# Layer 1 grouped-query attention: the two context query tiles of a head pair as one step

## The chip, the cores and the metric

The kernel runs on one core of one Trainium2 chip. The metric is the device time of one execution in microseconds (us); the median of three runs is quoted. Beside the timed runs there is one profiled execution, from which all traces here come. Engines are named as in the profile: PE (TensorE), DVE (VectorE), ACT (ScalarE), POOL (GpSimd), SP (the queue that issues most DMAs).

## The reference

A two-layer trunk of 512 latent tokens and 256 context tokens, 1024 channels wide. Each layer holds a mixer with four parallel branches (Fourier, convolution, grouped-query attention, differential attention) that are gated, summed and projected, and a SwiGLU sub-layer. What matters here:

```python
# grouped-query attention: 8 query heads of 64, 2 key/value heads
def gqa_attend(q, k, v):
    s = jnp.einsum("bhgqd,bhkd->bhgqk", q, k) * (HEAD_DIM ** -0.5)
    p = jax.nn.softmax(s, axis=-1)
    return jnp.einsum("bhgqk,bhkd->bhgqd", p, v)
# context stream (layer 1 only): reads only itself        -> 256 keys
# latent stream: reads all latent and all context tokens  -> 768 keys

def conformer_conv(z, w, bias, ln_g, ln_b):
    a, g = jnp.split(z, 2, axis=-1)
    u = a * jax.nn.sigmoid(g)
    y = depthwise_conv(u, w, 31 taps) + bias
    return jax.nn.silu(layer_norm(y, ln_g, ln_b))
```

In layer 1 both streams pass the mixer; in layer 2 the context has no queries of its own. The change touches only what is done for context queries, so layer 2 is computed as before.

## The kernel before

All large products are made of three matmuls each: operands are split into a high and a low part (fp32r), and high times high, high times low and low times high are summed in PSUM.

**Attention stage of layer 1.** It is one region written out by hand: inside `manual_schedule` the order of PE, DVE and ACT instructions is the order of the program text. Instructions of the code behind the region are placed by the scheduler and may stand between those of the region. The grouped-query loop (lines 1294 to 1360) runs over `steps`, pairs (j, t): four pairs of heads j, and for each six query tiles of 128, t = 0 to 3 latent (768 keys), t = 4 and 5 context (256 keys, `krange`, line 938). One step: transposes of the exponentials of head a = 0 (`transp`, L933, with a copy by ACT, L935, and a subtraction by DVE, L936, into `pt`); scores of the next step (`issue`, `scores` L904) and their row maximum (L910, L914); transposes of head a = 1; exponentials of the next step (L923); products with the values in two passes (L1343), high part of `pt` first; a transpose of the reciprocals of the row sums (L1345) into the same PSUM bank `pv`; and the eviction, two ACT copies (L1351), two DVE additions (L1354), one DVE multiplication (L1355); then `sums`, a reciprocal (L1286) and a POOL copy for the next step. PSUM has two banks with the tag "T" (`bank()`), two with "f" (`fbank()`), one "pv", and one scores tile of three banks ("S").

**Filler.** Between these pieces `fill.run(w)` emits matmuls of gate units and query projections (L607 to L609), so many by the planner's clock `clk` that `rate` times the weight w is used up. A latent step has weight 1, a context step 0.45 (`wt`). Generators that are due on the side are resumed in `pump` at the head of each `fill.run`, each at most once in 1.5 planned us (`GAP`): the rope of a projected query (`rot_rope`, L796 to L803), and later the layer norm of the convolution (`conv_ln`). In the last step but one of a head pair (p == nqt - 2) the next pair's query projection is finished: what is left of its rope is emitted at once, and `split_q` emits two ACT casts (L816) and two DVE subtractions (L820).

**Taps.** The depthwise convolution is 31 DVE instructions for each of four channel groups (L701 for 30 of them), kept in a queue `tapq`. Each grouped-query step takes two taps off the queue (`run_taps(NTS[l], True)`, NTS = 2) between the two passes of values; in the differential attention loop that follows, each of the first five of a head's six steps takes one (NTD = 1).

**What follows the taps.** At the head of the first differential step (hd, p) that finds the queue empty, `conv_ln` is parked as a side generator. It has 41 resumptions: for the latent range (512 columns) and then the context range (256) a sum over the groups, a matmul for the mean (L955), four subtractions (L957), squares (ACT, L962) and additions (L963), a matmul for the variance (L970), a small DVE instruction (L167), a power on POOL (L169), transposes (L977) and four multiplications (L980); then for four groups and two ranges an affine step and a tanh on ACT (L985, L987) and a DVE product (L989). In the last step of the loop, hd = 3 and p = 5, whatever is left is emitted at once, ahead of everything else of that step:

```python
if hd == 3 and p == nqt - 1:
    drain(cln)
    conv_split(0, 3)
```

`conv_split` makes high and low parts `yc` (ACT L998, DVE L999), which the convolution's gate units read right after the region (`dense(cu[:2], 2)`): each unit has, for two halves of the columns, 24 matmuls on the normalised input `h` (the gate) and 12 on `yc`.

## Time and profile before

| | us |
|---|---|
| median of 3 runs | 2641.51 |
| lowest, highest | 2640.91, 2641.99 |
| the profiled execution | 2644.01 |
| span of its trace, first to last instruction | 2642.2 |
| mean granted clock of PE, share of full speed | 0.993 |

The span lies 1.8 us inside the profiled execution's time, and that execution lies 2.5 us over the median. Read the profile from the share of PE's busy time first, then stretch by stretch: a stretch in which PE is busy throughout can't be shortened by another engine, and one in which it waits shows what ended last.

### The profile page before, as it was taken

Reading aid. Unit: us, or ns where it says so; the run is one execution under the profiler, and the core shown is the slowest. Engines: PE = TensorE matmul, PEld = TensorE weight load, DVE = VectorE, ACT = ScalarE, POOL = GpSimd, SP = SyncE. Lnnn points to the kernel's source line nnn. Section 1 sums busy time; section 2 is a strip of 40 time slices with the busy share of each in tenths; the row PEclk is TensorE's granted clock in tenths of the full one; section 3 lists DMA queues with packets and bytes.
Section 4 is the critical chain, followed back from the end, with each engine's and each line's share of the span. In section 5 each row is a group of like instructions: output and inputs, shape, how many; then the busy total and the mean of one; then the engine's idle time right before and its main releaser. Section 6 shows DMA issues by size and latency. Waiting matters only on the chain.

```text
span 2642.2 us, 38743 instructions
## 1 busy us (share of the span) xinstructions
PE 2564.4 (97%) x14651; PEld 2349.2 (89%) x14651; DVE 1710.8 (65%) x3042; ACT 1129.2 (43%) x2262; POOL 113.1 (4%) x179
## 2 busy tenths in 40 slices
PE   7999999999999999999999999999999999999998
PEld 5999889999999989999999988788888888988887
DVE  4967887777778667463353579987766635733335
ACT  5235555455522246212212254566655424623235
POOL 1000000010000000000000000100000000000000
PEclk8999999999999999999999999999999999999999
DMA  8211112222255355343353453111222234533334
GB/s 278 78 45 45 39 39 72 57 54 59 78 153 154 115 162 161 93 128 96 90 158 96 135 147 88 52 41 53 68 80 69 76 96 144 161 100 96 96 95 137
DMA packets 401760, 263.07 MB, mean 100 GB/s; under 512 B 15883, under 2 KB 369493, under 8 KB 401573
## 3 DMA queue, kind: packets, MB, share of 16 engines
q1 hardware_dynamic: 394292, 236.67, 30.3%
q0 software_dynamic: 7280, 23.93, 3.2%
q8 instruction: 115, 1.88, 0.3%
q14 instruction: 73, 0.59, 0.1%
HBM read 243.75 MB, written 8.91 MB: 96 GB/s over the span
## 4 chain that ended last, share of the span: by engine, by line
PE 84%; DVE 5%; ACT 4%; DMA 3%; issue 3%; POOL 0%; DVEq 0%; SPq 0%; POOLq 0%; ACTq 0%
PE pf L525 14%; PE pf L523 14%; PE pf L524 14%; PE pf L607 10%; PE pf L608 10%; PE pf L609 10%; PE pS L904 3%; PE pT L933 2%; PE pv L1343 2%; DMA ws<-in_w_ffn_dram 1%; PE pv L1432 1%; ACT e L923 1%; DVE wl L220 1%; DMA ws<-in_w_out_dram 1%; ACT wh L218 1%
## 5 line engine op out<-in xcount | busy, mean ns | idle before, releaser
L218 ACT CAST wh<-ws 128x512 fp32r<-128x512 f32 (+1 forms) x432 | 261.9, 608 | 582.8 <-PE pf L524 441.7
L523 PE MATMUL pf<-h,wh 128*128 128x384 f32 (+2 forms) x1360 | 468.4, 347 | 3.8 <-ACT tg L728 1.5
L524 PE MATMUL pf<-h,wh 128*128 128x384 f32 (+2 forms) x1360 | 468.4, 346 | 1.1 <-DVE h L181 1.1
L525 PE MATMUL pf<-h,wl 128*128 128x384 f32 (+2 forms) x1360 | 467.9, 346 | 0.5 <-DVE wl L220 0.4
L220 DVE TENSOR_TENSOR wl<-ws,wh 128x512 fp32r<-128x512 f32 (+1 forms) x432 | 289.5, 673 | 267.1 <-ACT wh L218 264.2
L607 PE MATMUL pf<-h,wh 128*128 128x384 f32 (+1 forms) x1280 | 459.1, 359 | 1.9 <-ACT tg L779 1.3
L609 PE MATMUL pf<-h,wl 128*128 128x384 f32 (+1 forms) x1280 | 449.0, 351 | 0.0
L608 PE MATMUL pf<-h,wh 128*128 128x384 f32 (+1 forms) x1280 | 447.8, 350 | 0.0
L523 PEld LDWEIGHTS pf<-h,wh 128*128 128x128 f32 x1360 | 254.9, 188 | 25.0 <-ACT h L180 2.8
L524 PEld LDWEIGHTS pf<-h,wh 128*128 128x128 f32 x1360 | 255.8, 188 | 20.9 <-DVE h L181 2.7
L525 PEld LDWEIGHTS pf<-h,wl 128*128 128x128 f32 x1360 | 255.5, 188 | 20.0 <-DVE wl L220 1.3
L563 ACT CAST wh<-ws 128x512 fp32r<-128x512 f32 x264 | 164.2, 623 | 236.1 <-PE pf L608 198.3
L607 PEld LDWEIGHTS pf<-h,wh 128*128 128x128 f32 x1280 | 241.4, 189 | 16.4 <-ACT tg L779 2.0
L608 PEld LDWEIGHTS pf<-h,wh 128*128 128x128 f32 x1280 | 241.6, 189 | 13.5 <-issue 0.7
L609 PEld LDWEIGHTS pf<-h,wl 128*128 128x128 f32 x1280 | 240.9, 188 | 13.4 <-issue 0.2
L570 DVE TENSOR_TENSOR wl<-ws,wh 128x512 fp32r<-128x512 f32 x264 | 181.1, 687 | 98.2 <-ACT wh L563 96.7
L701 DVE SCALAR_TENSOR_TENSOR ca<-ub,cols,ca 128x798 f32<-128x798 f32 (+1 forms) x240 | 215.3, 897 | 3.9
L525 PE MATMUL pf<-g,wl 128*128 128x384 f32 (+2 forms) x584 | 198.9, 341 | 1.3 <-DVE wl L220 1.1
L523 PE MATMUL pf<-g,wh 128*128 128x384 f32 (+2 forms) x584 | 199.2, 342 | 0.2
L130 DVE SCALAR_TENSOR_TENSOR wada<-wada,sil 128x512 f32<-128x512 f32 x224 | 162.5, 747 | 56.3 <-DMA wada<-in_w_ada_dram 55.0
L524 PE MATMUL pf<-g,wh 128*128 128x384 f32 (+2 forms) x584 | 197.7, 339 | 0.0
L935 ACT CAST pt<-pT 128x512 fp32r<-128x512 f32 (+1 forms) x216 | 91.9, 471 | 154.7 <-PE pT L933 154.2
(324 smaller groups left out, 4068.1 us busy)
## 6 DMA issues: line engine op xcount, KB each, us to landing
ws<-in_w_ffn_dram SPq DMA_DIRECT2D x284, 256.0 KB, 2.9
ws<-in_w_in_dram SPq DMA_DIRECT2D x248, 256.0 KB, 2.9
wada<-in_w_ada_dram SPq DMA_DIRECT2D x160, 256.0 KB, 3.0
ws<-in_w_out_dram SPq DMA_DIRECT2D x58, 256.0 KB, 2.9
ws<-in_w_ffn_dram SPq DMA_DIRECT2D x48, 192.0 KB
wada<-in_w_ada_dram SPq DMA_DIRECT2D x16, 512.0 KB, 6.8
khl<-khl POOLq DMA_DIRECT2D x40, 192.0 KB, 3.2
ws<-in_w_four_dram SPq DMA_DIRECT2D x16, 256.0 KB, 2.8
```

Source lines behind the costliest of these rows:

```text
L130: nc.vector.scalar_tensor_tensor(accs[r], w, s, accs[r], op0=ALU.mult, op1=ALU.add)
L218: nc.scalar.copy(wh[:, :n], st[:, :n])
L220: lastv[0] = nc.vector.tensor_sub(wl[:, :n], st[:, :n], wh[:, :n]).ins
L523: nc.tensor.matmul(o, lhsT=wh, rhs=xh(k), start=(k == 0), stop=False)
L524: nc.tensor.matmul(o, lhsT=wh, rhs=xl(k), start=False, stop=False)
L525: nc.tensor.matmul(o, lhsT=wl, rhs=xh(k), start=False, stop=(k == n - 1))
L563: nc.scalar.copy(wh, u.raw[len(u.wh)])
L570: nc.vector.tensor_sub(wl, u.raw[i], u.wh[i])
L607: nc.tensor.matmul(o, lhsT=wh, rhs=xh(k), start=(k == 0), stop=False)
L608: nc.tensor.matmul(o, lhsT=wh, rhs=xl(k), start=False, stop=False)
L609: nc.tensor.matmul(o, lhsT=wl, rhs=xh(k), start=False, stop=(k == nk - 1))
L701: nc.vector.scalar_tensor_tensor(a, u, w, a, op0=ALU.mult, op1=ALU.add)
```

## The change

For layer 1 the list of steps becomes `gsteps`, five to a head pair: t = 0 to 3 as before, and t = 4 for both context tiles. Its weight is 0.9, so `rate` is the same. The merged step has eight score matmuls of 256 columns into one scores tile, one row maximum over four blocks, four exponentials, transposes of four 128-column blocks into one bank for each head, eight value matmuls into the whole `pv` bank, the reciprocals' transposes in a bank of their own (`sbT`, tag "T"), and one eviction for both tiles. Two taps are still taken off the queue in each step. In layer 2 `npt` is four and all steps are of the old kind.

```diff
+                npt = nqt if last else 5
+                gsteps = [(j, t) for j in range(4) for t in range(npt)]
+
+                def gw(t):
+                    return 1.0 if t < 4 else 0.9
+
+                fill.rate = (8 * cost(36, halves) + 3 * cost(24, halves)) / (sum(gw(t) for _, t in gsteps) + 3.0)
...
                 def issue(i):
-                    j, t = steps[i]
-                    ko, nk = krange(t)
-                    S = scores(qbox[j], qbox["k"], (j // 2, j // 2), t, ko, nk)
+                    j, t = gsteps[i]
                     rq = qs[j][1]
-                    return row_max(S, nk, rq[:, 2 * t:2 * t + 2])
+                    if t < 4:
+                        S = scores(qbox[j], qbox["k"], (j // 2, j // 2), t, 0, NTOK)
+                        return row_max(S, NTOK, rq[:, 2 * t:2 * t + 2])
+                    S = sbank()
+                    for u in range(2):
+                        for a in range(2):
+                            o = S[:, a, u * CT:(u + 1) * CT]
+                            for h_ in range(2):
+                                clk[0] += CT / 2400.0
+                                nc.tensor.matmul(o, lhsT=qbox[j][:, a, X + u * P:X + (u + 1) * P],
+                                                 rhs=qbox["k"][h_][:, j // 2, X:NTOK], start=(h_ == 0), stop=(h_ == 1))
+                    nm = smp.tile([P, 16], F32, tag="ccol", name="nm4", bufs=1)[:, :4]
+                    nc.vector.reduce_max(nm, S[:, :, :2 * CT].rearrange("p a (u k) -> p a u k", u=2), axis=AX.X,
+                                         negate=True)
...
+                    return S, None, rq, nm
+
+                def gexps(S, nk, scale, nm):
+                    if nk is not None:
+                        return exps(S, nk, scale, nm)
+                    ss = smp.tile([P, 16], F32, tag="sil", name="ss4", bufs=1)[:, :4]
+                    es = []
+                    for a in range(2):
+                        e = etile(2 * CT, "e")
+                        for u in range(2):
+                            c_ = 2 * a + u
+                            nc.scalar.activation(e[:, u * CT:(u + 1) * CT], S[:, a, u * CT:(u + 1) * CT], AF.Exp,
+                                                 bias=nm[:, c_:c_ + 1], scale=scale[:, 8 + 2 * u + a:9 + 2 * u + a],
+                                                 accum_out=ss[:, 2 * u + a:2 * u + a + 1])
+                        es.append(e)
+                    return es, ss
...
-                    if p == nqt - 2 and j < 3:
+                    if p == npt - 2 and j < 3:
                         forced[0] = True
                         fill.finish(qu[j])
                         forced[0] = False
                         sq_ = split_q(qs[j + 1][0], NT, qbox, j + 1)
                         next(sq_)
-                        fill.run(wt(t) * GF[1])
+                        fill.run(gw(t) * GF[1])
                         drain(sq_)
...
                     for w in range(2):
                         if w:
                             run_taps(NTS[l], True)
-                            fill.run(wt(t) * GF[2])
+                            fill.run(gw(t) * GF[2])
+                        if two:
+                            for u, w_ in ((0, 0),) if w == 0 else ((0, 1), (1, 0), (1, 1)):
+                                for kt in range(2):
+                                    nc.tensor.matmul(pvs[:, u * 256:(u + 1) * 256], lhsT=vg[:, 4 + kt, j // 2],
+                                                     rhs=pt[:, w_, 2 * u + kt], start=(kt == 0 and w_ == 0),
+                                                     stop=(kt == 1 and w_ == 1))
+                            continue
...
-                    nc.tensor.transpose(pvs[:, 256:384], sb.rearrange("p a d -> p (a d)"), ident)
+                    nu = 2 if two else 1
+                    sbT = bank() if two else pvs[:, 256:384]
+                    for u in range(nu):
+                        nc.tensor.transpose(sbT[:, u * P:(u + 1) * P],
+                                            sb[u].rearrange("p a d -> p (a d)"), ident)
...
                     for a in range(2):
-                        nc.scalar.copy(y[64 * a:64 * a + 64, lo:lo + P], pvs[64:128, a * P:a * P + P])
+                        nc.scalar.copy(yv[64 * a:64 * a + 64], pv4[64:128, :, a])
                     for a in range(2):
-                        yv = y[64 * a:64 * a + 64, lo:lo + P]
-                        nc.vector.tensor_add(yv, yv, pvs[0:64, a * P:a * P + P])
-                    nc.vector.tensor_mul(y[:, lo:lo + P], y[:, lo:lo + P], pvs[:, 256:384])
+                        yw = yv[64 * a:64 * a + 64]
+                        nc.vector.tensor_add(yw, yw, pv4[0:64, :, a])
+                    nc.vector.tensor_mul(y[:, lo:lo + nu * P], y[:, lo:lo + nu * P], sbT[:, :nu * P])
```

## Rows read from the trace of the kernel before

**Rows 1.** The page, busy time and share of the span of each engine.
```profile
PE 2564.4 (97%) x14651; PEld 2349.2 (89%) x14651; DVE 1710.8 (65%) x3042; ACT 1129.2 (43%) x2262; POOL 113.1 (4%) x179
```
**Rows 2.** Stretches: start:end, length, PE, PEld, DVE, ACT, POOL busy, PE clock, DMA, GB/s.
```profile
264.00:276.00 12.00, 8.93 (x50) 7.06 (x49) 11.42 (x21) 7.66 (x18) 0.29 (x1) 1.00 0.08 24
314.00:330.00 16.00, 12.89 (x74) 10.78 (x73) 13.57 (x29) 8.28 (x21) 0.91 (x3) 1.00 0.12 33
370.00:384.00 14.00, 9.95 (x53) 7.87 (x52) 12.73 (x23) 9.02 (x22) 0.29 (x1) 0.96 0.07 20
384.00:386.00 2.00, 2.00 (x8) 1.81 (x8) 1.75 (x5) 0.58 (x2) 0.29 (x1) 0.50 0.45 131
560.00:606.00 46.00, 42.40 (x257) 40.47 (x256) 37.12 (x73) 29.11 (x59) 4.61 (x6) 1.00 0.25 64
630.00:676.00 46.00, 46.00 (x284) 45.71 (x283) 28.29 (x52) 27.23 (x57) 2.07 (x4) 1.00 0.26 70
```
**Rows 3.** Waits of PE, 205 to 450 us: total us, times, longest.
```profile
PE pv L1343 <- DVE pt L936: 3.8, 5, 1.0
PE pv L1343 <- DVE ss L1286: 3.7, 3, 1.4
PE pS L904 <- DVE qhl L820: 1.7, 3, 0.8
```
**Rows 4.** Timeline, ACT, first head pair: start, us, instruction, [idle before and releaser].
```profile
257.03 0.51 ACT L779 ACTIVATE tg<-pf 128x384 f32<-128x384 f32 x1
...
263.46 1.68 ACT L816 CAST qhl<-qe 64x768 fp32r<-64x768 f32 x2
```
**Rows 5.** Groups by form, 205 to 430 us: busy us, mean ns of one | idle before.
```profile
L701 DVE SCALAR_TENSOR_TENSOR ca<-ub,cols,ca 128x798 f32<-128x798 f32 x45 | 47.1, 1047 | 0.9
...
L910 DVE TENSOR_REDUCE nm<-pS 128x2 f32<-128x1536 f32 x16 | 28.0, 1753 | 1.8 <-PE pS L904 1.8
...
L796 ACT COPY rot<-qe 32x512 f32<-32x512 f32 x12 | 7.4, 618 | 0.2
...
L910 DVE TENSOR_REDUCE nm<-pS 128x2 f32<-128x512 f32 x8 | 5.4, 680 | 0.0
```
**Rows 6.** Timeline, DVE: first and last of eight taps behind grouped-query attention; `conv_ln` begins.
```profile
473.04 1.05 DVE L701 SCALAR_TENSOR_TENSOR ca<-ub,cols,ca 128x798 f32<-128x798 f32 x1
...
557.52 1.04 DVE L701 SCALAR_TENSOR_TENSOR ca<-ub,cols,ca 128x798 f32<-128x798 f32 x1
...
561.86 1.40 DVE L951 TENSOR_TENSOR cs<-cs,ca 128x512 f32<-128x512 f32 x2
```
**Rows 7.** Timeline, inside `conv_ln`.
```profile
576.04 0.16 DVE L167 TENSOR_SCALAR var<-pT 128x4 f32<-128x4 f32 x1 [1.21 <-PE pT L970]
...
578.03 0.60 PE L977 MATMUL pT<-ident,r 128*128 128x128 f32 x4
...
578.67 1.88 DVE L980 TENSOR_TENSOR ca<-ca,pT 128x512 f32<-128x512 f32 x3 [1.86 <-PE pT L977]
...
584.87 1.07 DVE L957 TENSOR_TENSOR ca<-ca,pT 128x256 f32<-128x256 f32 x3
```
**Rows 8.** Groups by form, 560 to 725 us, end of `conv_ln`.
```profile
L985 ACT ACTIVATE ca<-ca,cols 128x512 f32<-128x512 f32 x4 | 3.3, 821 | 0.0
...
L987 ACT ACTIVATE ct<-ca 128x512 f32<-128x512 f32 x4 | 2.5, 633 | 0.1
...
L985 ACT ACTIVATE ca<-ca,cols 128x256 f32<-128x256 f32 x4 | 2.4, 610 | 0.0
...
L987 ACT ACTIVATE ct<-ca 128x256 f32<-128x256 f32 x4 | 1.7, 417 | 0.1
```
**Rows 9.** Timeline, end of the attention stage.
```profile
712.02 0.34 PE L607 MATMUL pf<-h,wh 128*128 128x384 f32 x1
...
712.39 3.41 ACT L998 CAST yc<-ca 128x512 fp32r<-128x512 f32 x8
...
717.49 0.44 PE L607 MATMUL pf<-yc,wh 128*128 128x384 f32 x1 [0.36 <-ACT tg L779]
```

More of the change, by code (lines that the diff above doesn't have):

```diff
@@ L1269, in block_kernel @@
                 fill.nx = dunits(0)
-                fill.rate = (8 * cost(36, halves) + 3 * cost(24, halves)) / (sum(wt(t) for _, t in steps) + 3.0)
+                npt = nqt if last else 5
[3 more added lines that the diff above has]
+                fill.rate = (8 * cost(36, halves) + 3 * cost(24, halves)) / (sum(gw(t) for _, t in gsteps) + 3.0)
                 fill.b = -fill.chunk()
@@ new lines, in issue @@
+                    nm = smp.tile([P, 16], F32, tag="ccol", name="nm4", bufs=1)[:, :4]
+                    nc.vector.reduce_max(nm, S[:, :, :2 * CT].rearrange("p a (u k) -> p a u k", u=2), axis=AX.X,
+                                         negate=True)
+                    sc = rq[:, 8:12].rearrange("p (u a) -> p a u", a=2)
+                    nc.vector.tensor_tensor(nm.rearrange("p (a u) -> p a u", a=2),
+                                            nm.rearrange("p (a u) -> p a u", a=2), sc, op=ALU.mult)
@@ L1285, in sums @@
                 def sums(ss):
                     nc.vector.reciprocal(ss, ss)
-                    sb = smp.tile([P, 2, 64], F32, tag="sb", name="sb", bufs=2)
-                    nc.gpsimd.tensor_copy(sb, ss.unsqueeze(2).to_broadcast([P, 2, 64]))
-                    return sb
+                    res = []
+                    for u in range(0, ss.shape[-1], 2):
+                        sb = smp.tile([P, 2, 64], F32, tag="sb", name="sb", bufs=2)
+                        nc.gpsimd.tensor_copy(sb, ss[:, u:u + 2].unsqueeze(2).to_broadcast([P, 2, 64]))
+                        res.append(sb)
@@ L1291, in block_kernel @@
+                    return res
                 for w in PRE[:3]:
@@ L1294, in block_kernel @@
                 fill.run(PRE[3])
-                es, ss = exps(*nm_)
+                es, ss = gexps(*nm_)
                 fill.run(PRE[4])
                 sb = sums(ss)
-                for i, (j, t) in enumerate(steps):
-                    p = i % nqt
-                    more = i + 1 < len(steps)
+                for i, (j, t) in enumerate(gsteps):
+                    p = i % npt
+                    more = i + 1 < len(gsteps)
                     if p == 0:
@@ L1303, in block_kernel @@
                         yg.append(y)
-                    ko, nk = krange(t)
-                    k0, nkt_ = ko // P, nk // P
+                    two = t == 4
+                    nkt_ = 4 if two else 6
                     pt, pt5 = pttile()
@@ L1309, in block_kernel @@
                         nm_ = issue(i + 1)
-                        fill.run(wt(t) * GF[0])
+                        fill.run(gw(t) * GF[0])
                     else:
@@ L1318, in block_kernel @@
                     if more:
-                        es, ss = exps(*nm_)
-                    if p == nqt - 2 and j < 3:
+                        es, ss = gexps(*nm_)
+                    if p == npt - 2 and j < 3:
                         forced[0] = True
@@ L1330, in block_kernel @@
                     else:
-                        fill.run(wt(t) * GF[1])
+                        fill.run(gw(t) * GF[1])
                     if not more:
@@ L1342, in block_kernel @@
                         for kt in range(nkt_):
-                            nc.tensor.matmul(pvs[:, :256], lhsT=vg[:, k0 + kt, j // 2], rhs=pt[:, w, kt],
+                            nc.tensor.matmul(pvs[:, :256], lhsT=vg[:, kt, j // 2], rhs=pt[:, w, kt],
                                              start=(kt == 0 and w == 0), stop=(kt == nkt_ - 1 and w == 1))
-                    nc.tensor.transpose(pvs[:, 256:384], sb.rearrange("p a d -> p (a d)"), ident)
+                    nu = 2 if two else 1
@@ L1346, in block_kernel @@
+                    sbT = bank() if two else pvs[:, 256:384]
+                    for u in range(nu):
+                        nc.tensor.transpose(sbT[:, u * P:(u + 1) * P],
+                                            sb[u].rearrange("p a d -> p (a d)"), ident)
                     clk[0] += nkt_ * 0.214
-                    area[0] = pvs[:, 384:396]
-                    fill.run(wt(t) * GF[3])
+                    if not two:
+                        area[0] = pvs[:, 384:396]
+                    fill.run(gw(t) * GF[3])
@@ L1354, in block_kernel @@
-                        nc.vector.tensor_add(yv, yv, pvs[0:64, a * P:a * P + P])
-                    nc.vector.tensor_mul(y[:, lo:lo + P], y[:, lo:lo + P], pvs[:, 256:384])
+                        yw = yv[64 * a:64 * a + 64]
+                        nc.vector.tensor_add(yw, yw, pv4[0:64, :, a])
+                    nc.vector.tensor_mul(y[:, lo:lo + nu * P], y[:, lo:lo + nu * P], sbT[:, :nu * P])
                     if more:
                         sb = sums(ss)
-                    fill.run(wt(t) * GF[4])
@@ L1359, in block_kernel @@
-                    if p == nqt - 1 and j < 2:
+                    fill.run(gw(t) * GF[4])
+                    if p == npt - 1 and j < 2:
                         park1(yg, j, "ygd")
```

2 lines of the change are left out of this document (added).

## The prediction

> **What bounds the kernel now.** I read the page first: PE is busy for 97% of the span [rows 1], so only time in which PE waits can be won, 2642.2 - 2564.4 = 77.8 us in all. Then I read the stretches around the context steps. Of the four pairs of heads, three are followed by another pair, and at each of those places PE has holes: it is busy for 8.93 of 12.00 us, 12.89 of 16.00 and 9.95 of 14.00 [rows 2], which leaves 3.07, 3.11 and 4.05 us, 10.2 us together. Behind the third the clock falls: 0.96 over its stretch and 0.50 over the next 2 us [rows 2]; the first is 0.04 x 14 = 0.6 us, the second 1.0 us, some 1.6 us lost. Three kinds of wait carry them, 9.2 us between 205 and 450 us [rows 3]; they lie in these three stretches. So the most that the merge can give where it is made is 10.2 + 1.6 = 11.8 us.
>
> Who is late there? DVE, which is busy for 11.42 of 12.00 us and 12.73 of 14.00 [rows 2]; PE waits for its subtractions, for its eviction of the value bank (the reciprocal named in rows 3 stands directly behind that eviction) and for the next queries' low part [rows 3].
>
> Then I looked at what the removed steps carry besides attention. Each step takes two taps off the queue. In the trace eight taps are left when the grouped-query loop ends, and `conv_ln` starts a little after the last of them [rows 6].
>
> **What the merge removes and adds at a boundary.** Matmul columns, transposes and filler stay as they were. DVE loses two taps of 1.047 us, 2.09 us [rows 5]. Two maxima over 512 numbers (0.680 each) become one over 1024; from 512 to 1536 the price goes from 0.680 to 1.753, so 1024 is estimated at 1.22, a gain of 0.14 us [rows 5]. Fewer evictions and subtractions give some tenths more. That is at least 2.2 us of DVE work less against holes of 3 to 4 us, three times.
>
> Three things go against it. First, `split_q` moves one step earlier, into the last latent step, ahead of `fill.run`. Its two casts take 1.68 us on ACT [rows 4]; what is queued behind them on ACT is the filler's tanh, which in the trace ran at 257.03 in just that step [rows 4] and releases one of two banks that PE's next gate needs. Today PE does not wait there; then the tanh ends some 3 us later (four exponentials in place of two, then the casts) and PE stands up to 1.5 us. Second, the reciprocals' transposes now hold a "T" bank until DVE's last product of the eviction, behind two taps and a maximum, and PE's next step wants that bank within two filler pieces; I estimate 1 to 2 us. Third, the earlier `split_q` meets an unfinished rope in the third pair: by the planner's clock (5.10 planned us per weight, one resumption in 1.5) the third projection is parked late in step t = 2, and two resumptions of its rope are still due in t = 3. They are emitted at once: two copies of 0.618 us [rows 5] and three DVE products of about 0.63 each (1.88 for three [rows 7]), 3.1 us in series ahead of the casts, while PE has about 5 us of other work; I estimate 2 to 3 us more of a wait for the queries.
>
> Sum for the loop: between 11.8 us won (all holes and the clock) and 3 us lost (DVE saves nothing that PE sees, and the rope's 3 us are added). Playing the queues forward in order through the first boundary, PE comes to the next pair's second scores less than 1 us sooner than in the trace, since a wait for the "T" bank stands where the other waits were. So I take 1 us won at each of the first two, nothing at the third, and half a microsecond for the last pair: 2.5 us, nearer to the lower end.
>
> **What the merge moves: eight taps.** With twenty steps in place of twenty-four, forty taps are taken and not forty-eight; sixteen are left and not eight. The differential loop takes five for each head, so the queue is empty after the first step of the last head, hd = 3, where it was empty after p = 2 of the second. `conv_ln` is therefore parked at hd = 3, p = 1. A latent step advances the planner's clock by 1.28 (scores) + 0.64 (transposes) + 4.23 (filler: two gate units, 23.04, over weights of 5.45), and by 1.92 for values in every second step; with four calls to `fill.run` in a step and one resumption in 1.5, three are made in a latent step, one or two in a context step. By p = 5 nine or ten of 41 have been made: the sum and squares of the latent range. The other 31 are emitted at once at the head of the last step. In the trace they ran beside the second and third head.
>
> The batch is a chain. From the end of what DVE must do first (about 713.5 on the old time axis): the small DVE instruction and the power, 2.0 us to the transposes (576.04 to 578.03); 0.64 to the first product and four of 0.63, 3.1 us [rows 7]; for the context range three additions of about 0.4, 1.25; the mean's matmul and four subtractions of 0.36, 0.6 + 1.43 = 2.05 [rows 7]; three more additions and the last square, 1.45; the variance's matmul, small instruction and power again, 3.05; transposes and the first product, 0.9. That is 13.8 us. Then ACT, which has eight pairs of affine and tanh, 3.3 + 2.5 + 2.4 + 1.7 = 9.9 us [rows 8]; it can do one pair of 1.45 us during the second power, so 8.45 more. `conv_split` begins at about 735.7 and not at 712.39 [rows 9], 23.3 us later.
>
> What can PE do meanwhile? In the trace the first gate's 24 matmuls were already pulled ahead of the last step (712.02), and the first product with `yc` came at 717.49 [rows 9]; it waits for casts and subtractions of four groups, so it would end about 21 us later than it did. PE can pull forward the gates of two more halves (two "f" banks and two gate tiles allow three in all), 24 matmuls each, which take about 4.15 us (between 712.02 and 717.49 stand 24 of them and some short transposes [rows 9]), 8.3 us; the last step's values, 1.4 us; and `conv_ln`'s own matmuls, 2.8 us, which are no longer done earlier. That leaves PE idle for 21 - 12.5 = 8.5 us. After holes of 4 us the clock was at 0.50 for some time and cost 1.6 us [rows 2]; that is added: 10 us. Casts and tanhs of the pulled-forward gates that stand in ACT's chain add up to 2 us. I take 12 us; the lower end is 8.5, the upper end 18.3 + 2 = 20 us, if no further gate is pulled forward.
>
> A rule of the Trainium skill bears on this. The trace shows the order: ACT's casts for `yc` follow the region's last exponentials directly [rows 9], in the order of the text. PSUM — Partial Sum Buffer, section Engine vs sequencer instructions, says that the queues of ScalarE and VectorE are strictly first in, first out and that matmuls start in program order. By that rule nothing behind the batch on ACT or DVE can pass it; if it could, the term of 12 us would be zero and the sum 12 us lower.
>
> The batch also leaves the place where it was. In 560 to 606 us PE is idle for 46.00 - 42.40 = 3.6 us, while the same stretch of the next head, 630 to 676, has none [rows 2]. I count these 3.6 us as won; the eight taps that come there instead are 1.05 us each in steps where DVE is busy for 28.29 of 46.00 us [rows 2], and cost nothing unless several queue up.
>
> **Sum.** -2.5 (loop) - 3.6 (second head) + 12 (end of the stage) = +5.9 us. The profiled execution, 2644.0, would become 2649.9; against the median of 2641.5, 2.5 us lower, I forecast 2647.4.
>
> Of the clock: the row of 0.50 follows the holes before it [rows 2]. TensorE: Matmul & The Clock Gate, section HAM oscillation, says that gaps in matmul work bring the clock back to its lower level, so that the next work starts cold; the trace agrees (0.50 in that row), and without it the sum would be about 1.6 us lower.
>
> **Rivals.** (1) The holes at the boundaries go for the most part, since DVE has more than 2 us less to do at each and the bank waits don't come: 10 us won there, 12 lost at the end, 3.6 won: 2641.5 - 1.6 = 2639.9. For it speaks DVE's share of the stretches, against it that PE's waits have three different causes there. (2) PE finds no more gates to pull forward, because their weights or banks are not ready: 20 us at the end: 2641.5 - 2.5 - 3.6 + 20 = 2655.4. For it speaks that only one half was pulled forward in the trace; against it that no more was needed. (3) The end is hidden after all, because the resumptions come faster than I count, or PE has other work: then only the gains stay, 2.5 to 11.8 and 3.6, so 2626 to 2635; it needs the batch to be at most about 10 us long, where I count 23. (4) The merge doesn't do what it says at the boundary: DVE stays late, the new bank wait takes the place of the old ones, nothing is won there; 2649.9. The forecast's other side is rival 1 or 3; slower than before decides itself at the point where PE's idle time at the end is over 6 us plus what the boundaries give.
>
> **How the numbers follow.** Chances: forecast with rival 4 beside it (2643 to 2652) 0.5, rival 1 0.2, rival 2 0.2, rival 3 0.1. The likeliest gives 2647.4. The range takes in rival 1 with somewhat more gain and rival 2 with 2 us more: 2637 to 2658. A change of 0.2% (5.3 us) is about what can be told from none. Slower by more: rival 2 whole and somewhat over half of the forecast's case, 0.5. Within: the rest of that and most of rival 1, 0.38. Faster: rival 3 and a little of rival 1, 0.12.
>
> **What would show it.** In the profile of the changed kernel: eight taps fewer before the differential loop and sixteen behind it; `conv_ln` beginning in the last head; its affine steps and tanhs in one unbroken run on ACT just before the casts to `yc`; a hole of about 8 us or more in PE before the first product with `yc`, and the clock at 0.50 behind it; no hole in the second head; at the boundaries fewer waits for `pt` and the value bank, and new ones of the transposes (L933) for DVE. The prediction is wrong if the run on ACT is short or PE is busy beside it, or if the holes at the boundaries vanish wholly.

## The result, and the profile after

The changed kernel takes 2657.26 us (median of 4 runs, 2655.32 to 2658.07), the kernel before 2641.21 (2640.73 to 2641.99; the three runs of the table above and one more): a ratio of 1.0061 with a 95% interval of 1.0049 to 1.0074, 16.05 us more. The span of its profiled execution is 2656.2 us and the mean granted clock 0.989. The forecast was 2647.4 with a range of 2637 to 2658, slower being the likeliest; the time lies in the range, 0.7 us under its upper end and 9.9 us over the forecast.

The page of the changed kernel, busy time and share of each engine:

```profile
PE 2562.8 (96%) x14651; PEld 2351.2 (89%) x14651; DVE 1708.8 (64%) x3010; ACT 1127.8 (42%) x2246; POOL 112.8 (4%) x179
```

Against [rows 1] PE has as many instructions and 1.6 us less busy time; DVE has 32 instructions less, ACT 16. No engine has more to do. What was lost is time in which PE stands or runs at the lower clock, so the question is where. This table is made from the timelines of the two kernels: for six marks the time since the first score matmul (L904) of the grouped-query loop. "Loop end" and "head 1 to 3" are the first transposes of the values (L891) with which the differential loop enters a head, "first yc" the first product of PE with `yc`, "gates" the first cast by ACT of the gated sum (`mg`), just behind the last gate unit. The two profiled executions differ by 14.0 us in span; the first scores come at 212.02 us before and at 209.08 after, behind a part whose text is the same, and the table leaves that part out. How far such marks can be trusted shows in a kernel of the experiments whose loop is that of the changed one (resume_fast): its loop end is at 239.2 instead of 239.7.

| mark, us since the first scores | before | after | after, longer by | of which in this section |
|---|---|---|---|---|
| loop end | 240.8 | 239.7 | -1.1 | -1.1 |
| head 1 | 312.7 | 311.3 | -1.4 | -0.3 |
| head 2 | 387.9 | 379.9 | -8.0 | -6.6 |
| head 3 | 457.9 | 448.4 | -9.5 | -1.5 |
| first yc | 505.5 | 520.1 | +14.6 | +24.1 |
| gates | 712.9 | 729.0 | +16.1 | +1.5 |

The loss is in one section, the last head of the differential loop, and a little behind it.

**That section.** First the taps of the changed kernel and the start of `conv_ln` (timeline, DVE; start, us, instruction). There are sixteen taps behind the loop; the first, the last, and the sum that begins `conv_ln`:

```profile
468.70 1.04 DVE L701 SCALAR_TENSOR_TENSOR ca<-ub,cols,ca 128x798 f32<-128x798 f32 x1
...
673.32 1.05 DVE L701 SCALAR_TENSOR_TENSOR ca<-ub,cols,ca 128x798 f32<-128x798 f32 x1
...
677.20 0.69 DVE L948 TENSOR_TENSOR cs<-ca 128x512 f32<-128x512 f32 x1
```

In [rows 6] the last of eight was at 557.52 and `conv_ln` began a little behind it; now it begins some 115 us later, with one head left. What of it is not done by then is emitted in one batch ahead of the last step. The timeline of that batch (PE and ACT, with the idle time before an instruction and its releaser):

```profile
707.12 0.34 PE L609 MATMUL pf<-h,wl 128*128 128x384 f32 x1
707.30 0.60 PE L977 MATMUL pT<-ident,r 128*128 128x128 f32 x4
...
711.82 0.67 PE L955 MATMUL pT<-cs,mean 128*128 128x256 f32 x2 [3.92 <-DVE cs L951]
...
715.48 0.98 PE L970 MATMUL pT<-ones,vs 128*128 128x1 f32 x4 [2.99 <-DVE vs L963]
...
717.57 0.69 PE L977 MATMUL pT<-ident,r 128*128 128x128 f32 x2 [1.10 <-POOL r L169]
718.05 0.63 PE L933 MATMUL pT<-ident,e 128*128 128x128 f32 x2
...
727.29 0.58 ACT L985 ACTIVATE ca<-ca,cols 128x256 f32<-128x256 f32 x1
728.20 0.42 ACT L987 ACTIVATE ct<-ca 128x256 f32<-128x256 f32 x1 [0.33 <-DVE ca L989]
728.52 1.74 ACT L998 CAST yc<-ca 128x512 fp32r<-128x512 f32 x4
...
729.18 0.69 PE L607 MATMUL pf<-yc,wh 128*128 128x384 f32 x1 [7.91 <-ACT yc L998]
```

It is read from the bottom: PE stands 7.91 us until ACT casts `yc`, and ACT casts it directly behind the last of its affine steps and tanhs. Above that PE stands 3.92, 2.99 and 1.10 us at three of `conv_ln`'s own matmuls, each one link of its chain. The transposes of the last attention step (L933, 718.05) stand behind them on PE, and so does all else of that step.

The same in stretches (start:end, length, PE, PEld, DVE, ACT, POOL busy, PE clock, DMA, GB/s):

```profile
702.00:708.00 6.00, 5.90 (x39) 5.62 (x37) 1.82 (x7) 1.68 (x6) 1.39 (x1) 1.00 0.29 87
708.00:712.00 4.00, 0.18 (x1) 0.21 (x2) 3.60 (x7) 0.00 (x0) 0.00 (x0) 1.00 0.00 0
712.00:718.00 6.00, 1.91 (x8) 1.45 (x8) 2.76 (x8) 3.22 (x7) 0.70 (x1) 0.57 0.00 0
718.00:722.00 4.00, 2.09 (x10) 1.63 (x8) 2.60 (x7) 2.17 (x4) 0.03 (x1) 0.50 0.02 4
722.00:729.00 7.00, 0.00 (x0) 0.00 (x0) 3.28 (x6) 5.96 (x12) 0.82 (x1) 0.50 0.00 1
729.00:731.00 2.00, 1.78 (x4) 1.27 (x5) 1.92 (x5) 2.00 (x7) 0.00 (x0) 0.50 0.32 88
731.00:733.00 2.00, 2.00 (x9) 2.00 (x9) 2.00 (x6) 1.92 (x5) 0.00 (x0) 0.50 0.79 242
```

From 702 to 733 PE is idle for 31.00 - 13.86 = 17.1 us. From 712 on it runs at 0.57 and 0.50, so that of 7.8 us of work some 3.8 us are due to the clock (0.43 of 1.91 and half of 5.87). Its share at 729 to 733, 1.9 us, falls behind the first product with `yc`. Over the whole section, from the first transposes of head 3 to the first product with `yc`, the stretches of the kernel before and of the changed one are

```profile
669.93:717.49 47.56, 47.20 (x308) 46.09 (x306) 35.06 (x70) 25.96 (x63) 1.70 (x2) 1.00 0.17 48
```

```profile
657.52:729.18 71.66, 53.26 (x331) 50.16 (x329) 50.57 (x103) 35.47 (x79) 4.64 (x5) 0.89 0.10 30
```

PE's idle time grows from 0.36 to 18.40 us, by 18.0: the 16.9 from 702 us to the first product with `yc`, and 1.2 of a wait of L955 for `pt` earlier in the head. Its busy time grows by 6.1: `conv_ln`'s six matmuls, which were done in the second head before and took 4.2 us there (1.02 + 1.02 + 0.60 + 0.59 + 0.58 + 0.43), and the clock's other 1.9. That is the +24.1. The rest of the clock's share is the +1.5 behind it.

**The head before.** This is the stretch of the changed kernel that answers to 560:606 in [rows 2]:

```profile
556.00:602.00 46.00, 46.00 (x287) 45.54 (x286) 28.86 (x51) 25.55 (x54) 3.78 (x6) 1.00 0.26 69
```

PE was busy for 42.40 us there and is now busy throughout: the 3.6 us of holes are gone. Some 2.5 us of them lay in the second head (PE's idle time in it was 2.65 us and is now 0.15), and with the 4.2 us of `conv_ln`'s matmuls they make the -6.6. The last hole, 1.08 us at 600 us of the kernel before, lay already in the third head and is most of its -1.5.

**The grouped-query loop.** Waits of PE from 205 us to the loop's end (total us, times, longest), to be read against [rows 3]:

```profile
PE pf L607 <- ACT tg L779: 7.5, 3, 4.8
PE pT L933 <- DVE yg L1408: 3.9, 3, 1.4
...
PE pv L1384 <- DVE pt L936: 0.4, 1, 0.4
```

All three waits of [rows 3] are gone or nearly so, 9.2 us. In their place stand the two that the prediction named, 11.4 us: for the tanh of a gate, and of the transposes for the eviction that now holds a "T" bank. So PE waits more than before: from the first scores to the loop's end it is idle for 13.6 us where it was 11.7. The loop is 1.1 us shorter all the same, since PE's busy time in it is 226.1 us and was 229.1, for the same number of matmuls and in spite of more time at the lower clock. Why the same matmuls show 3 us less busy time the runs don't tell. At the first pair and at the third the wait for the tanh comes about like this (timeline; PE and ACT):

```profile
255.99 1.69 ACT L816 CAST qhl<-qe 64x768 fp32r<-64x768 f32 x2
257.70 0.49 ACT L779 ACTIVATE tg<-pf 128x384 f32<-128x384 f32 x1
258.25 0.45 PE L607 MATMUL pf<-h,wh 128*128 128x384 f32 x1 [1.34 <-ACT tg L779]
...
360.66 1.24 ACT L796 COPY rot<-qe 32x512 f32<-32x512 f32 x2
363.98 1.68 ACT L816 CAST qhl<-qe 64x768 fp32r<-64x768 f32 x2 [2.08 <-DVE qe L803]
365.69 0.49 ACT L779 ACTIVATE tg<-pf 128x384 f32<-128x384 f32 x1
366.23 0.69 PE L607 MATMUL pf<-h,wh 128*128 128x384 f32 x1 [4.83 <-ACT tg L779]
```

The tanh stands behind the casts of the next queries. At the third pair these wait for a rope that had not been finished (copies, three products on DVE, then the casts), and PE stands 4.83 us; over 360 to 384 us its clock is 0.86.

### The profile page after: what moved, and what is told of

Read it like the earlier page. It is cut to its first block, busy times and chain, and to the rows that moved or that the text cites. A ratio compares the mean times of both kernels' runs of the same rounds, so it can differ in the third digit from the quotient of the medians.

```text
span 2656.2 us, 38681 instructions
## 1 busy us (share of the span) xinstructions
PE 2562.8 (96%) x14651; PEld 2351.2 (89%) x14651; DVE 1708.8 (64%) x3010; ACT 1127.8 (42%) x2246; POOL 112.8 (4%) x179
## 4 chain that ended last, share of the span: by engine, by line
PE 85%; DVE 5%; ACT 4%; issue 3%; DMA 3%; POOL 0%; DVEq 0%; POOLq 0%; SPq 0%; ACTq 0%
PE pf L525 14%; PE pf L524 14%; PE pf L523 14%; PE pf L607 10%; PE pf L608 10%; PE pf L609 10%; PE pS L904 3%; PE pT L933 2%; DMA ws<-in_w_ffn_dram 1%; PE pv L1389 1%; PE pv L1485 1%; ACT e L923 1%; DVE nm L910 1%; ACT wh L218 1%; ACT pt L935 1%
## 5 line engine op out<-in xcount | busy, mean ns | idle before, releaser
L563 ACT CAST wh<-ws 128x512 fp32r<-128x512 f32 x264 | 164.0, 623 | 239.7 <-PE pf L608 203.3
L608 PEld LDWEIGHTS pf<-h,wh 128*128 128x128 f32 x1280 | 242.4, 189 | 13.6 <-issue 0.6
```

Of the source, the lines that this page charges most:

```text
L563: nc.scalar.copy(wh, u.raw[len(u.wh)])
L608: nc.tensor.matmul(o, lhsT=wh, rhs=xl(k), start=False, stop=False)
```

## The experiments

Every kernel was timed against the kernel before on the same chip. The ratio is this kernel's time by that of the kernel before, with its 95% interval. "Since the first scores" is the measure of the table above.

### Is it the batch at the end, and does one tap decide it?

One tap more in the merged step of the first pair, in the changed kernel:

```diff
-                            run_taps(NTS[l], True)
+                            run_taps(3 if two and j == 0 else NTS[l], True)
```

> The changed kernel with one tap more: the first merged step takes three taps off the queue and not two, so fifteen are left for the differential loop. Theory T (the loss is the batch of the layer norm of the convolution at the end of the attention stage): the queue is then empty one step earlier, at the end of the third head instead of within the fourth, the planner's clock gives 39 of 41 resumptions ahead of the last step, and the whole loss of some 23 us at the end goes: 2635 to 2642 us. Rival R (the loss comes from the boundaries in the grouped-query loop, tanh and bank waits): one tap changes nothing, 2655 to 2659 us. Rival S (the loss grows with the number of taps left, DVE work that is only moved): one of eight, 2655 us.

Measured: 2643.02 us, ratio 1.0005 (0.9995 to 1.0014): 14.2 us less than the changed kernel for one DVE instruction of 1.05 us that is taken earlier, and 1 us above the range of theory T. With 15 taps left and five taken in a head, the queue is empty one step before the end of the third head, and `conv_ln` is parked there. Its start on DVE, three of its eight pairs on ACT, the casts and the first product with `yc` (timeline):

```profile
633.91 0.68 DVE L948 TENSOR_TENSOR cs<-ca 128x512 f32<-128x512 f32 x1
...
666.49 0.82 ACT L985 ACTIVATE ca<-ca,cols 128x512 f32<-128x512 f32 x1
...
687.86 0.61 ACT L985 ACTIVATE ca<-ca,cols 128x256 f32<-128x256 f32 x1
...
708.30 0.61 ACT L985 ACTIVATE ca<-ca,cols 128x256 f32<-128x256 f32 x1
...
709.63 2.58 ACT L998 CAST yc<-ca 128x512 fp32r<-128x512 f32 x6
...
714.20 0.44 PE L607 MATMUL pf<-yc,wh 128*128 128x384 f32 x1 [1.10 <-ACT tg L779]
```

The eight pairs begin 1.7 to 8.3 us apart, among other work, and PE waits 1.10 us where it waited 7.91. The loop is as long as in the changed kernel (239.4 and 239.7 us), the third head takes 77.2 us instead of 68.6, and the section to the first `yc` 49.9 instead of 71.7. From the loop's end to the first `yc` that makes 267.3 us, where the kernel before takes 264.6: `conv_ln` in the third head isn't free. All the same, the loss at the end hangs on whether the queue is empty at one step, not on how many taps there are.

The other half of the question: the same loss without any merge. In the kernel before no taps are taken in the first context step, so that forty are taken in the loop as in the changed kernel:

```diff
-                            run_taps(NTS[l], True)
+                            run_taps(0 if t == 4 else NTS[l], True)
```

> The kernel before, with its two context steps for each pair unmerged, but no taps in the first of them: forty taps are taken in the loop and sixteen left, as in the changed kernel. Theory T: the loss at the end of the stage appears without any merge; +20 to +24 us there, less 5 us of waits that leave the second head, less up to 2 us at each of three boundaries where DVE has two taps less: 2650 to 2660 us. Rival R: no change or faster, 2632 to 2642 us.

Measured: 2650.25 us, ratio 1.0033 (1.0021 to 1.0045). The section to the first `yc` takes 72.2 us against 47.6, as in the changed kernel, and PE's waits in it are the same: 7.9 for the casts of `yc`, 3.9, 3.0, 1.2 and 1.1. So the loss at the end belongs to the eight taps alone. The run shows something else as well: its loop ends at 232.4 us since the first scores, 8.4 earlier than before. These are PE's waits from 205 to 450 us:

```profile
PE pS L904 <- DVE qhl L820: 1.7, 3, 0.8
PE pv L1343 <- ACT pt L935: 1.4, 3, 0.5
PE pv L1343 <- DVE pt L936: 0.8, 2, 0.7
...
PE pT L933 <- ACT e L923: 0.5, 2, 0.2
```

That is 4.4 us where the merged loop with as many taps has 7.5 + 3.9 + 0.4 = 11.8. PE's whole idle time in the two loops is 5.5 and 13.6 us, its busy time 226.9 and 226.1, and so the merged loop is 239.7 - 232.4 = 7.3 us longer. The two loops differ by the merge alone, so **the merge costs some 7 us where it is made, and what it seemed to give came from the taps that fell out with the removed steps.** Three more pairs of runs below, each with equal numbers of taps, say the same of the loop: 5.9 us (taps_in_merge against the kernel before), 6.1 (one_tap against before_41) and 6.4 (merged_shift against shift2).

The third of these puts the eight taps back where they were, in the merged steps, four in each:

```diff
-                            run_taps(NTS[l], True)
+                            run_taps(4 if two else NTS[l], True)
```

> The changed kernel with four taps in each merged step: forty-eight in the loop as in the kernel before, eight left. Theory T: the layer norm begins where it began before and the loss at the end goes; the boundaries keep the kernel's DVE work of before, so that the eviction that the transposes wait for comes about 2 us later at each of three: 2640 to 2648 us. Rival R: 2657 us or more.

Measured: 2650.6 us, ratio 1.0034 (1.0024 to 1.0044), above the range of theory T. The end is as before (47.6 us), and the loop is 7.0 us longer than in the changed kernel (246.7). Two taps of 1.05 us in each of four steps are 8.4 us of DVE, so most of it is seen by PE: the waits for the "T" bank grow from 3.9 to 9.6 us, those for the tanh stay as they are. PE's waits, 205 to 450 us:

```profile
PE pT L933 <- DVE yg L1408: 9.6, 3, 3.5
PE pf L607 <- ACT tg L779: 7.5, 3, 4.8
```

### Can the batch be spread over the last head instead?

In the changed kernel `conv_ln` is resumed at every chance, not once in 1.5 planned us:

```diff
-                                e[1] = clk[0] + gap
+                                e[1] = clk[0] + (e[2] if len(e) > 2 else gap)
...
-                        fill.park(cln, 0.0)
+                        fill.side.append([cln, clk[0], 0.0])
```

> The changed kernel, only that the layer norm of the convolution may be resumed at every call of the filler and not once in 1.5 planned us. By the planner's clock 17 of its 41 resumptions are then made ahead of the last step and not 9 or 10, so the batch is shorter by the latent range's variance and products, the context range's sum and subtractions, by my terms 2.0 + 3.1 + 1.25 + 2.05 + 0.6 = 9 us of the chain. Theory T: 8 to 12 us less than the changed kernel, 2645 to 2650 us. Rival (only all or nothing counts, or the loss is elsewhere): 2655 to 2658 us.

Measured: 2659.04 us, ratio 1.0067 (1.0052 to 1.0082); nothing is won, and the first product with `yc` comes at 519.9 us since the first scores, in the changed kernel at 520.1. The stretches of this kernel from 684 us on, and PE's waits from 670 to 735 us, show where it went:

```profile
684.00:692.00 8.00, 6.25 (x39) 5.77 (x38) 6.16 (x11) 5.27 (x11) 0.00 (x0) 1.00 0.01 2
692.00:700.00 8.00, 6.08 (x35) 5.82 (x34) 4.93 (x12) 2.40 (x7) 1.01 (x1) 0.85 0.11 33
```

```profile
PE pf L607 <- ACT yc L998: 7.9, 1, 7.9
...
PE pT L970 <- DVE pt L936: 1.9, 1, 1.9
PE pT L933 <- DVE ca L957: 1.7, 1, 1.7
```

In the changed kernel PE was busy for 8.00 of the second stretch's 8.00 us. The first links of the batch are done earlier, but PE stands at them, the last step begins later, and ACT's run of eight pairs stays behind it whole. That the context steps of a head have too little filler for these links is the likely reason, but no run tests it. One head was too short for `conv_ln`; begun at the end of the third head, ahead of the next head's projections, it was spread (one_tap).

### Can the merge's own cost be taken away?

With the tap of one_tap, the casts of the next queries are emitted behind `fill.run`, so that the gates' tanhs stand ahead of them on ACT:

```diff
                     if p == npt - 2 and j < 3:
...
+                        if not last:
+                            fill.run(gw(t) * GF[1])
                         sq_ = split_q(qs[j + 1][0], NT, qbox, j + 1)
                         next(sq_)
-                        fill.run(gw(t) * GF[1])
+                        if last:
+                            fill.run(gw(t) * GF[1])
                         drain(sq_)
```

> The kernel with one tap more, and in the last latent step of a pair (layer 1 only) the filler stands ahead of the casts of the next queries and not behind them, so the filler's tanh is not queued on ACT behind the casts. Theory: the three waits of the gate matmuls for the tanh (1.3, 1.3 and 4.8 us in the changed kernel) go, the queries come some 0.6 us later: 5 to 8 us less than with one tap more alone. Rival: the queries' low part becomes the wait in their place, 0 to 2 us less.

Measured: 2642.6 us, ratio 1.0003 (0.9993 to 1.0012), against 1.0005 for one_tap without it: no difference. The wait that it aims at goes, from 7.5 to 1.1 us. PE's waits, 205 to 450 us:

```profile
PE pT L933 <- DVE yg L1411: 4.7, 3, 2.9
PE pv L1387 <- DVE pt L936: 4.3, 3, 1.9
...
PE pf L607 <- ACT tg L779: 1.1, 1, 1.1
PE pS L904 <- DVE qhl L820: 1.0, 2, 0.6
```

Waits for `pt` (0.4 in one_tap, now 4.3) and for the queries (none in one_tap) take its place. The loop ends at 241.2 us, 1.8 later than in one_tap; PE's idle time in it is less (12.7 us against 13.6), but its busy time for as many matmuls is more (228.5 against 225.8), and why the rows don't tell.

Both bank and casts at once: the casts late as above, and the taps of the merged step taken behind `sums(ss)`, so that the eviction frees its "T" bank ahead of them:

```diff
                         if w:
-                            run_taps(3 if two and j == 0 else NTS[l], True)
+                            if not two:
+                                run_taps(NTS[l], True)
...
                     if more:
                         sb = sums(ss)
+                    if two:
+                        run_taps(3 if j == 0 else NTS[l], True)
```

> The merged kernel with one tap more, the casts behind the filler's tanh, and the merged step's taps behind its eviction. Theory (the merge's own loss is the tanh wait and the wait of the transposes for the bank of the reciprocals): the bank wait of 1.1 to 2.9 us at each of three boundaries goes too, 4 to 8 us less than casts late alone: 2634 to 2638 us. Rival: DVE has the same work at the same place, the wait goes to the next row maximum, 2640 to 2643 us.

Measured: 2643.29 us, ratio 1.0005 (0.9996 to 1.0015); the loop ends at 238.7 us. The wait for the bank is 3.8 us, that for `pt` 4.3. The waits moved and did not go; no order that was tried brings the merged loop near to the 232.4 us of the loop without a merge.

### Are the taps the thing to move?

The kernel before with forty-one taps in the loop, one in the first pair's first context step and none in the others':

```diff
-                            run_taps(NTS[l], True)
+                            run_taps((1 if j == 0 else 0) if t == 4 else NTS[l], True)
```

> The unmerged kernel with no taps in the first context step of a pair, but one in the first pair: forty-one taps in the loop, fifteen left. From the trace with forty taps, the grouped-query loop is 8.4 us shorter than in the kernel before and the loss stands at the end of the stage. Theory T2 (what the merge was to bring comes from the taps that it drops, and the end is lost only because the queue empties one step too late): the end is as in the kernel with one tap more, 2632 to 2636 us, and 7 us less than the merged kernel with one tap more. Rival: the end costs again what the loop wins, 2640 to 2646 us.

Measured: 2638.34 us, ratio 0.9986 (0.9977 to 0.9995). The loop ends at 233.3 us, as theory T2 has it, and the end of the stage is spread as in one_tap; against forty taps one tap wins 11.9 us here too, without a merge. But the time lies between the two ranges: from the loop's end to the first `yc` it takes 267.5 us, 2.9 more than in the kernel before.

With all forty-eight, two taken out of the first context step and one more in each of the first two latent steps:

```diff
-                            run_taps(NTS[l], True)
+                            run_taps(NTS[l] if last else (3, 3, 2, 2, 0, 2)[t], True)
```

> The unmerged kernel with all forty-eight taps in the loop, but none in the first context step of a pair and three in each of the first two latent steps: eight left, as before. Theory T2: the loop is 8 us shorter, since PE does not wait beside DVE in latent steps, and nothing else moves: 2632 to 2635 us. Rival (DVE's sum over the loop binds, not its place): 2640 to 2642 us.

Measured: 2634.32 us, ratio 0.9973 (0.9962 to 0.9983): **faster than both kernels, without the merge.** The loop ends at 233.5 us, 7.3 earlier than before, and each section behind it is as before within 0.2 us. PE's waits, 205 to 450 us, against the 9.2 us of [rows 3]:

```profile
PE pS L904 <- DVE qhl L820: 1.7, 3, 0.8
...
PE pv L1343 <- ACT pt L935: 1.4, 3, 0.5
PE pv L1343 <- DVE pt L936: 1.0, 2, 0.7
```

The wait for the value bank (3.7) is gone and that for `pt` falls from 3.8 to 1.0. What had been late at a boundary were two taps.

Two more arrangements, with three taps in each latent step and none in either context step, and with fifty-six taps:

```diff
-                            run_taps(NTS[l], True)
+                            run_taps(NTS[l] if last else (3, 3, 3, 3, 0, 0)[t], True)
```

> The unmerged kernel with forty-eight taps, three in each latent step and none in either context step. If DVE at the boundary still ends last in the second context step (two taps there in the earlier shifted kernel), 1 to 3 us less than that kernel's 2634.3 us; if only the first context step mattered, the same within 1 us.

Measured: 2636.74 us, ratio 0.9983 (0.9974 to 0.9993); the loop ends at 236.7 us, and there are waits for the value bank (0.9 us), for `pt` (1.6) and of the transposes for DVE (0.9), together 3.4 where the earlier shifted kernel has 1.0. Nothing is won over that kernel, so taps in the last two latent steps are not free either. The intervals of the two times overlap; the loops differ by 3.2 us.

```diff
-                            run_taps(NTS[l], True)
+                            run_taps(NTS[l] if last else (4, 4, 3, 3, 0, 0)[t], True)
```

> The unmerged kernel with fifty-six taps in the loop, none in the context steps: no tap is left, and the layer norm begins in the first differential step instead of the second head. What it costs by itself: in the kernel before it makes the second head 75.2 us long where heads without it have 68.6 to 71.9 us. Theory: beginning in steps rather than in the stretch of projections, its sums are spread over the first head, and its cost of 5 to 7 us falls to half: 2631 to 2635 us. Rival: DVE, with three and four taps in a latent step, now delays these steps: 2636 us or more.

Measured: 2644.69 us, ratio 1.0012 (1.0003 to 1.0022). That is 10.4 us more than with forty-eight taps in before_shift, and two things make it. The loop ends at 241.1 us, 7.6 later than there: PE's waits for DVE in it are 6.2 us against 2.7, as the rival said of three and four taps in a latent step. And with no tap left for the differential loop `conv_ln` is resumed in the first head, which takes 77.6 us instead of 71.9: PE waits there for links of it (L955, 1.3 and 1.1; L970, 1.2), and then 3.8 us for copies of the values (L891) that ACT makes, where the kernel before has at most 1.9. From the loop's end to the first `yc` it is 268.4 us against 264.6, so an earlier beginning of `conv_ln` is not cheaper.

### The merge with its taps in place

The changed kernel with forty-eight taps, none in the merged step:

```diff
-                            run_taps(NTS[l], True)
+                            run_taps(NTS[l] if last else (3, 3, 3, 3, 0)[t], True)
```

> The merged kernel with all forty-eight taps in the loop, three in each latent step and none in the merged step, so that the layer norm begins as in the kernel before. It differs from the unmerged kernel with shifted taps (2634.3 us) by the merge alone. Theory M (the merge has a loss of its own: the gate's wait for the tanh behind the casts, 7.5 us at three places, and the transposes' wait for the reciprocals' bank): 2637 to 2642 us. Rival (with DVE free at the boundary the merge is even or wins): 2630 to 2635 us.

Measured: 2644.52 us, ratio 1.0011 (1.0002 to 1.0020), even above the range of theory M. And with the casts late as well (the edit of casts_late):

> The same with the casts of the next queries behind the filler's tanh in the last latent step. Theory M: the wait for the tanh goes, 1 of 7.5 us is left; with DVE free of taps in the merged step nothing takes its place: 2632 to 2636 us, within 3 us of the unmerged kernel with shifted taps. Rival: as in the earlier pair of runs with and without late casts, other waits come in its place, and the gain is under 2 us.

Measured: 2643.68 us, ratio 1.0007 (0.9998 to 1.0017), as the rival said. The end of the stage is 47.6 us in both, as before. The loops end at 243.1 and 246.0 us against 236.7 for the same three taps in every latent step without the merge (shift2): with equal taps the merge costs 6.4 us in the loop, and 2644.52 - 2636.74 = 7.8 us in the time, both taken beside the same runs of the kernel before. The tanh's wait is still 8.2 us in the first of the two; in the second it is 1.1, and those for `pt` and the value bank are 4.7 and 2.3. It was not tried whether the merged step could do without the "T" bank for its reciprocals, or with a third such bank.

## Why the prediction was right, and where it was mis-sized

**The loop (-2.5 taken, bounds -11.8 and +3; -1.1 measured).** The costs were named rightly. The tanh behind the casts was put at "up to 1.5 us" for a pair: 1.34 at the first. The bank of the reciprocals at 1 to 2: 3.9 in three times, the longest 1.4. The third pair's rope at 2 to 3 us more: 4.83 against 1.34 is 3.5. The maximum over 1024 was estimated at 1.22 us and took 1.214. What the prediction did not see is that the gain which stood against these costs was that of the two taps, and nearly all of it: it counted 2.09 of "at least 2.2" us as the taps' in its sum of DVE's work, but took them as part of the merge. Before_40 tells them apart: -8.4 for the taps, +7.3 for the merge. That the loop came within 1.4 us of the forecast is in part luck: PE's waits were to become less by some microseconds, and its idle time grew by 1.9; the loop is shorter by PE's busy time, 3.0 us less, of which the prediction has no step.

**The second head (-3.6 taken).** Right: PE's idle time in the second and third head falls from 2.65 + 1.38 to 0.15 + 0.15 us, 3.7 less. The other 4.3 us of the -6.6 and -1.5 are busy time, `conv_ln`'s matmuls that are done later.

**The end of the stage (+12 taken, bounds 8.5 and 20).** This is the term that was mis-sized. `conv_ln` did begin in the last head, its pairs run unbroken on ACT into the casts of `yc`, PE stands 7.91 us ahead of the first product, and the clock is at 0.50 behind. But in this section PE is idle for 18.0 us more than before and not for 8.5, and it loses 3.8 to the clock and not 1.6: 21.8 us together where 12 were taken. The step that failed is "PE can pull forward the gates of two more halves", 8.3 us of work. As in the kernel before, one half's 24 matmuls were pulled ahead of the last step (to 707.12) and no more; and the last step's values, another 1.4 us of the sum, came at 731.99, behind the first product with `yc`. So 9.7 us of work were not there to fill the time. The first `yc` is also 24.1 us later and not 21, which adds 3.1, while `conv_ln`'s matmuls (4.2 us and not 2.8) and the clock (1.9) fill 3.3 more: 8.5 + 9.7 + 3.1 - 3.3 = 18.0. That is rival 2's mechanism, which had a chance of 0.2 and gave 2655.4. The time lies in the range only because the range took in that rival; the likeliest case, two more halves, did not happen. Why no second half was pulled forward is not settled: no run tries more banks or more gate tiles. The chain's length was near: 24.95 us from the small DVE instruction (L167, 703.57) to the casts (728.52) where 13.8 + 8.45 = 22.25 were worked out, since its first transposes waited behind the gates (3.7 us from the small instruction and not 2.0), and ACT waits 0.33 us or more for DVE's product in every group.

The prediction's rule from the Trainium skill (PSUM — Partial Sum Buffer, section Engine vs sequencer instructions: the queues of ScalarE and VectorE keep strict order, matmuls start in program order) agrees with the rows of the batch: ACT's casts at 728.52 follow the last tanh at 728.20, though their first inputs had been finished at about 720.3 (L989 of the first group, 719.62 + 0.68), and PE's transposes for attention stand behind those of `conv_ln` at 718.05.

**The sum.** In the prediction's order: -1.1 (loop), -3.7 (the holes of the second and third head), and at the end of the stage +18.0 idle and +1.9 + 1.5 from the clock, with -0.3 in the first head, makes +16.3; `conv_ln`'s matmuls, -4.3 and +4.2, cancel. Between the traces' marks it is 16.1, and 16.05 between the medians. Of rival 4 one half holds, the new waits took the place of the old ones at the boundaries; the other half, that DVE stays late, doesn't: the wait for `pt` is 0.4 us where it was 3.8.

## What to carry to other kernels

Work that is taken "so many in each step" moves when the number of steps changes; before such a change, count where the queue runs empty and what is parked behind it, since one instruction more or less can decide whether a chain of 25 us is spread or done in one piece. When a step is merged, test what was removed with it by itself: here taking the side work off the late step, without the merge, gave 7 us, and the merge took as much back. A chain of dependent small steps needs other work between its links: spread over the end of one head and the next it was hidden (one_tap), resumed more often within one head it was not (resume_fast).

## What the runs showed of the chip that was not expected

The granted clock stayed at its lower level (0.50) from 718 to 733 us, through four stretches: PE was busy there for 2.09 of 4.00 us, 0.00 of 7.00, 1.78 of 2.00 and 2.00 of 2.00; in the 4.00 us before it fell PE had been busy for 0.18. So a hole costs more than its length: of the 3.8 us that the clock took, 1.9 fell in the 4 us behind the last hole. That agrees with what the Trainium skill says of gaps (TensorE: Matmul & The Clock Gate, section HAM oscillation — how this bites in real kernels: work behind a gap starts cold). In the grouped-query loop the third pair's wait of 4.83 us goes with a clock of 0.86 over 24 us, while the kernels whose longest wait there is 0.8 us (before_40 and before_shift) keep 1.00 over the same place.
